# 27 unit pairs and three dense units in the grouped-query stage, two raw weight loads moved into the value stage, and the last quarter's order

## The chip, the core and the metric

The kernel runs on one NeuronCore of one Trainium2 chip. The metric is device time of one launch in microseconds (us). The engines are called as in the profile: PE is the matmul engine (its weight loads are PEld), DVE the vector engine, ACT the scalar (activation) engine, POOL the GpSimd engine, and SP the engine whose queue issues most DMAs. PSUM holds matmul results (8 banks of 128 x 512 float32), SBUF everything else.

## The reference

One encoder block over 1024 tokens of width 1024, in float32:

```
h = rms_norm(x, g_pre)
a_qkv, bq, bk, bv, mq, ga, gb, gm, mg = split(h @ w_in)
oa = three dilated sliding-window attentions (8 heads each), merged by their log-denominators
ob = grouped-query attention: 8 query heads over 2 key/value heads, qk rms-norm, axial rotary
om = cross-attention into 256 memory tokens
y_i = (o_i * silu(g_i)) @ w_br_i                      (i = a, b, m)
merged = sum_i sigmoid(mg_i + b_merge_i) * y_i
out = x + rms_norm(merged @ w_out, g_post)
```

The part of `w_in` that matters here is cut into *units*: 128 output columns, a 128 x 1024 block of raw weights. 24 units (`U_M`) make the merge gates `mg`, 12 (`U_G`) the silu gates, 24 the rotary queries and keys of the sliding-window branch.

## The kernel before, in words

Each float32 operand is split into two fp32r parts, high and low (`split`, lines 105 to 107: ACT copies the high part, DVE subtracts it to get the low part). A product is three matmul passes: high-high, high-low and low-high. `hh` and `hl` are the two parts of the normalised input for all 1024 tokens.

A unit can be computed in two ways:

- **Dense** (`dense`, lines 139 to 149, by `add_unit`): for each half of the tokens 8 blocks x 3 passes, so 48 matmuls of 512 columns a unit, with a raw load of 512 KB and one split. Dense units of the merge gates (`add_filler`) serve as filler inside attention stages: `weave` interleaves the unit's matmuls with those of the attention by a table of nominal costs, and gives the filler out evenly over the attention's cost. `FILL` lists which merge-gate units are done this way; the first runs in the cross-attention stage, the others (`FILL[1:]`) in the grouped-query stage.
- **In pairs**, by a Strassen-type scheme with seven products (lines 925 to 1395): two units are multiplied at once with seven products of 12 matmuls, 84 matmuls instead of 96. The operands are sums of halves of the raw weights (`weight_sum`: S1 to S4; POOL forms them, DVE for pair 1), their splits (`block_of`, `own_blocks`) and sums of halves of the input (T1 to T4, prepared in the value stage and split on the way, `split_block`). A pair needs both its raw weights, `BL[n][0]` and `BL[n][1]`, which `load_pair` fetches through SP's queue. Merge-gate units that are not in `FILL` come as the last pairs.

The stages follow each other on PE, whose order is fixed by the program: start and key/value projection, cross-attention with queries, the grouped-query stage ("B", lines 651 to 792), the value stage (16 steps and 28 steps of 12 matmuls, line 997), the pairs (line 1109), the sliding-window attention with the branch projections woven in (line 1312), and the output projection (line 1892), which again uses seven products (`prod_o`).

**Grouped-query stage.** It works on 16 items (8 token tiles x 2 key/value heads) of 8 steps each. Step n issues a row-maximum matmul (`row_max`, line 705) into one of three PSUM tiles `tr`, which DVE reduces (line 706); two steps after the last row of an item a small transpose (`shift`, line 713, with DVE line 714) brings the maxima into the score operand; twelve steps later come the scores (lines 723, 724), whose exponentials ACT writes to `bp` (line 726); POOL sums the eight `bp` tiles of an item one after the other (lines 728, 730); after the item's eighth score and two more, `pv` issues 16 matmuls of values (line 739), and one step later `final` sums the denominators with two matmuls (line 126) whose operands `blh` and `bll` are a split of POOL's sum by ACT and DVE. `q_prep` turns the next tile's queries (line 679), copied by ACT and DVE (lines 682 to 686), and uses a `tr` tile as well. ACT, DVE and POOL are ordered by a scheduler in this stage, PE by the program.

**From the value stage to the pairs.** From the value stage on all engines run in program order. `START` gives the first products: (0,1), (0,2), (0,4), (0,3), (1,1), (0,5), (1,4) and so on, where (n, x) is product x of pair n. `own_blocks(1)` splits pair 1's first raw weights for (1,1). The raw weights of pair 0 are loaded inside the value stage, both into `wr` tiles (two buffers); those of pair 1 after it, since the second one lies in memory of the pool `sr`, which replaces the value stage's pool `vp`. The value stage's results leave through `vr` tiles (seven buffers) and DMAs that SP and ACT issue.

**Last quarter.** Row block 3 ends the program: its first half of rows, (3,0), is scaled and sent by `send_part`, while product (3,"5") and the two 256-column cuts of product (3,"7") finish the second half, (3,1): `evac_o` and `piece(0)`, `piece(1)` bring them from PSUM (lines 1911 and 2052), ACT squares them (line 1904), and after mean (lines 1918, 1920) and POOL's root (line 1924) the last `send_part`s (line 1953) send them.

Of the kernel before, what the change touches and what calls it, by code (L numbers as in the profile page):

```python
# [8 lines left out]
F32 = mybir.dt.float32  # L9
# [6 lines left out]
S = 1024  # L16
NT = 8
P = 128
# [32 lines left out]
def block(ctx: ExitStack, tc: tile.TileContext, x, xT, memT, cst, msk, bcst, tabA, gpost,  # L51
          wu, wv, wb, wmem, wbr, wout, out):
    nc = tc.nc
# [4 lines left out]
    wp = ctx.enter_context(tc.tile_pool(name="wp", bufs=2))  # L58
# [749 lines left out]
    tbp, tb = pool("tb")  # L808
    tab = [tb.tile([P, S], F32, name=f"tab{j}") for j in range(2)]
    vpp, vp = pool("vp")  # L810
    t23p, t23 = pool("t23", "right")
# [11 lines left out]
    def rs():  # L823
        return vp.tile([P, 512], F32, name="vr", bufs=7)

# [22 lines left out]
    x_load(0)  # L848
    rl = vp.tile([P, 64], F32, name="rl")
    VR = {}  # L850
# [93 lines left out]
    def load_pair(n, u):  # L944
        if u == 0 or n == 0:
            BL[n][u] = wp.tile([P, 1024], F32, name="wr", bufs=WR)
        else:
            BL[n][u] = sr.tile([P, 1024], F32, name="rw", bufs=2)
        nc.sync.dma_start(BL[n][u], wu[pairs[n][1][u]])
# [36 lines left out]
    for n, (i, e, k) in enumerate(steps_v):  # L986
# [30 lines left out]
        if 6 <= n < 20 and n % 4 == 3:  # L1017
            x_blocks(n // 4 - 1)
            if n < 19:
                x_load(n // 4)  # L1020
        if n == 4:
            nc.sync.dma_start(rl, lbd.rearrange("h (a b) -> (h a) b", b=64))
        if n == 8:
# [14 lines left out]
        if n == FIRST + 16:  # L1038
            load_pair(0, 0)
            load_pair(0, 1)  # L1040
        if n == FIRST + 21:
            own_blocks(0)
# [25 lines left out]
    p1, v_, y_ = [sr.tile([P, 512], F32, name=f"sp{j}") for j in range(3)]  # L1068
    load_pair(1, 0)
    load_pair(1, 1)  # L1070
# [148 lines left out]
    def m_load(tile_):  # L1219
        nc.sync.dma_start(tile_, od[2, len(MB)])  # L1220
        MB.append(tile_)
# [7 lines left out]
    def tasks(n, x):  # L1229
# [8 lines left out]
        for m, nm in blocks:  # L1238
            block_of(m, nm)
        for nm, k in {(0, "1"): [("T2", 2), ("T2", 3)], (0, "2"): [("T3", 0)]}.get((n, x), ()):  # L1240
            split_block(nm, k)
        j = {(0, "2"): 1, (0, "4"): 2, (0, "3"): 3, (1, "4"): 4}.get((n, x))
        if j:
# [23 lines left out]
        if n == last - 1 and x in "46" or n == last and x == "1":  # L1267
            if x != "6":
                m_load(wp.tile([P, S], F32, name="wr", bufs=WR))
            if x != "1":  # L1270
                m_load(sr.tile([P, S], F32, name="rw", bufs=2))
        if n == last and x in "4352":
# [84 lines left out]
    for n, nm in order:  # L1357
        prod(n, nm)
        if (n, nm) == (0, "4"):
            own_blocks(1)  # L1360
            for j in (1, 2, 3):
                split_block("T3", j)
# [584 lines left out]
    def gain(n, u, c):  # L1947
        r = RES[n, u]
        V.tensor_tensor(r[:, c], r[:, c], gp[:, c], op=OP.mult)

    def send_part(n, u, c, queue_):
        T, r = n + 4 * u, RES[n, u]
        V.scalar_tensor_tensor(r[:, c], r[:, c], SS[n, u][:, 3:4], XT_[T][:, c], op0=OP.mult, op1=OP.add)
        queue_.dma_start(out[T * 128:T * 128 + 128, c], r[:, c])
# [91 lines left out]
    gain(3, 0, hi)  # L2046
    send_part(3, 0, lo, nc.sync)
    send_part(3, 0, hi, nc.sync)
    evac_o(*before)

    def piece(e):
        V.tensor_tensor(res[:, quarter[e]], d[e], u2[:, quarter[e]], op=OP.add)
        square(3, 1, 2 * e, res[:, quarter[e]])

    piece(0)
    gain(3, 1, hi)
    mean(3, 1, (1, 0))
    piece(1)
    gain(3, 1, quarter[0])
# [21 lines left out]
LA_T, LA_P = 2, 3  # L2081
FILL = (16, 17, 18, 19, 20, 21)
GATES = ((2, 2), (2, 3), (1, 0), (1, 1), (1, 2), (1, 3), (0, 0), (0, 1), (0, 2), (0, 3))
# [110 lines left out]
```

## Time and profile before

| what | before |
|---|---|
| median of 3 runs (lowest to highest) | 1412.65 us (1411.01 to 1413.41) |
| the profiled execution | 1410.94 us, span 1409.2 us |
| mean granted PE clock | 0.998 |
| PE busy | 1382.1 us, 98% of the span |
| DVE, ACT, POOL busy | 987.5, 678.9, 556.5 us |
| chain that ended last | PE 88%, DVE 5%, ACT 2%, issue 2% |
| grouped-query stage | about 218 to 438.5 us of the span |
| value stage | 438.5 to 558 us |
| pairs | 558 to 1057 us |
| sliding-window attention, output projection | 1057 to 1325 us, 1325 to 1409 us |

Times in the rows of the profile count from the span's start; the span leaves out 1.74 us of the profiled execution. PE's busy time overstates its work, since each matmul is shown with its whole passage (about 389 ns) while the next one follows after about 227 ns: the distance from start to start is what one costs. A small gap between two matmuls hides inside that overlap.

### The profile page before, as it was taken

Reading aid. Unit: us, or ns where it says so; the run is one execution under the profiler, and the core shown is the slowest. Engines: PE = TensorE matmul, PEld = TensorE weight load, DVE = VectorE, ACT = ScalarE, POOL = GpSimd, SP = SyncE. Lnnn points to the kernel's source line nnn. Section 1 sums busy time; section 2 is a strip of 40 time slices with the busy share of each in tenths; the row PEclk is TensorE's granted clock in tenths of the full one; section 3 lists DMA queues with packets and bytes.
Section 4 is the critical chain, followed back from the end, with each engine's and each line's share of the span. In section 5 each row is a group of like instructions: output and inputs, shape, how many; then the busy total and the mean of one; then the engine's idle time right before and its main releaser. Section 6 shows DMA issues by size and latency. Waiting matters only on the chain.

```text
span 1409.2 us, 21232 instructions
## 1 busy us (share of the span) xinstructions
PE 1382.1 (98%) x7487; PEld 1106.4 (79%) x7487; DVE 987.5 (70%) x1774; ACT 678.9 (48%) x1450; POOL 556.5 (39%) x437
## 2 busy tenths in 40 slices
PE   7999999999999999999999999999999999999997
PEld 7799986666666888788888888888887777777886
DVE  7765567677663387789787777755666666868977
ACT  6553355666653454544223222344456766742453
POOL 0515603766763422177455565423310011345410
PEclk9999999999999999999999999999999999999999
DMA  6342011011005673565455665665667576746613
GB/s 232 105 133 63 28 58 54 28 34 35 23 27 185 242 260 110 182 223 215 123 167 164 178 180 158 211 225 187 213 210 251 181 225 199 243 121 226 229 61 135
DMA packets 107067, 215.80 MB, mean 153 GB/s; under 512 B 19952, under 2 KB 49872, under 8 KB 106960
## 3 DMA queue, kind: packets, MB, share of 16 engines
q1 hardware_dynamic: 93184, 200.68, 44.2%
q10 hardware_dynamic: 13776, 13.77, 2.8%
q8 instruction: 59, 0.97, 0.3%
q14 instruction: 48, 0.39, 0.1%
HBM read 141.73 MB, written 60.09 MB: 143 GB/s over the span
## 4 chain that ended last, share of the span: by engine, by line
PE 88%; DVE 5%; ACT 2%; issue 2%; POOL 1%; DMA 1%; SPq 0%; POOLq 0%; ACTq 0%; DVEq 0%
PE s L1109 34%; PE d L1312 9%; PE s L997 6%; PE s L1892 4%; PE ov L739 4%; PE s L1479 3%; PE d L1542 3%; PE d L144 3%; PE d L146 3%; PE d L148 3%; PE tr L705 2%; PE s L723 2%; PE s L724 2%; PE d L997 2%; PE d L540 2%
## 5 line engine op out<-in xcount | busy, mean ns | idle before, releaser
L1109 PE MATMUL s<-T,ch 128*128 128x512 f32 x912 | 215.2, 389 | 1.7 <-ACT sp L1174 1.7
L1109 PEld LDWEIGHTS s<-T,ch 128*128 128x128 f32 x912 | 171.1, 188 | 37.7 <-ACT sp L1174 2.1
L730 POOL TENSOR_TENSOR bl<-bl,bp 128x512 f32<-128x512 f32 x96 | 123.7, 1288 | 48.5 <-ACT bp L726 42.5
L107 DVE TENSOR_TENSOR ch<-sf,ch 128x512 fp32r<-128x512 f32 x102 | 92.5, 914 | 62.7 <-ACT ch L106 62.6
L1109 PE MATMUL s<-hh,ch 128*128 128x512 f32 x408 | 129.8, 389 | 0.0
L1312 PE MATMUL d<-hh,wh 128*128 128x512 f32 x384 | 126.8, 399 | 1.0 <-DVE wl L1318 1.0
L706 DVE TENSOR_REDUCE bn<-tr 128x1 f32<-128x512 f32 x128 | 85.4, 686 | 19.6 <-PE tr L705 18.2
L726 ACT ACTIVATE bp<-s 128x512 f32<-128x512 f32 x128 | 76.0, 597 | 45.0 <-PE s L724 43.3
L1142 POOL TENSOR_TENSOR o<-o,rc 128x1024 f32<-128x1024 f32 x24 | 61.9, 2580 | 70.6 <-DMA o<-rs 48.3
L1109 PEld LDWEIGHTS s<-hh,ch 128*128 128x128 f32 x408 | 76.6, 188 | 15.9
L1174 ACT ACTIVATE sp<-s 128x512 f32<-128x512 f32 x52 | 31.1, 598 | 115.2 <-PE s L1109 94.5
L1312 PEld LDWEIGHTS d<-hh,wh 128*128 128x128 f32 x384 | 72.0, 188 | 17.2 <-DVE wl L1318 1.6
L1319 POOL TENSOR_TENSOR acc<-acc,wl 128x512 f32<-128x512 f32 x32 | 56.8, 1778 | 68.2 <-DVE wl L1318 68.0
L1109 PE MATMUL s<-hh,wl 128*128 128x512 f32 x208 | 81.0, 390 | 1.4 <-DVE wl L107 1.4
L1109 PE MATMUL s<-hl,wh 128*128 128x512 f32 x208 | 80.9, 389 | 0.0
L1109 PE MATMUL s<-hh,wh 128*128 128x512 f32 x208 | 80.9, 389 | 0.0
L1109 PE MATMUL s<-hl,ch 128*128 128x512 f32 x204 | 79.4, 389 | 0.0
L106 ACT ACTIVATE wh<-wr 128x1024 fp32r<-128x1024 f32 (+1 forms) x64 | 56.1, 878 | 46.9 <-PE d L1312 12.0
L144 PE MATMUL d<-hh,wh 128*128 128x512 f32 x192 | 76.6, 399 | 1.7 <-DVE fth L223 1.7
L1497 ACT ACTIVATE pra<-pra,sts 128x192 f32<-128x192 f32 (+2 forms) x176 | 77.4, 442 | 1.6 <-DVE sts L1489 1.6
L1312 PE MATMUL d<-hl,wh 128*128 128x512 f32 x192 | 77.8, 405 | 0.0
L146 PE MATMUL d<-hl,wh 128*128 128x512 f32 x192 | 76.6, 399 | 0.0
(422 smaller groups left out, 3596.9 us busy)
## 6 DMA issues: line engine op xcount, KB each, us to landing
wr<-in_wu SPq DMA_DIRECT2D x39, 512.0 KB, 6.4
rw<-in_wu SPq DMA_DIRECT2D x25, 512.0 KB, 4.9
o<-rs SPq DMA_DIRECT2D x96, 128.0 KB, 2.3
qkd<-o SPq DMA_DIRECT2D x24, 512.0 KB, 6.3
wl<-thd SPq DMA_DIRECT2D x24, 512.0 KB, 5.3
thd<-rs ACTq DMA_DIRECT2D x36, 256.0 KB, 2.7
aq<-qkd SPq DMA_DIRECT2D x12, 512.0 KB, 4.6
ak<-qkd SPq DMA_DIRECT2D x12, 512.0 KB, 6.0
```

The source lines that it names most:

```text
L107: V.tensor_tensor(dst_l, src, dst_h.bitcast(F32), op=OP.subtract)
L144: PE.matmul(dst, wh[:, k, :], hh[k][:, t], start=k == 0, stop=False)
L146: PE.matmul(dst, wh[:, k, :], hl[k][:, t], start=False, stop=False)
L706: fp["last"] = V.tensor_reduce(st[i]["n"][:, j, c:c + 1], s, axis=AX.X, op=OP.min)
L726: A.activation(pp, s, AF.Exp, scale=-1.0)
L730: G.tensor_tensor(lsum[i % 2], lsum[i % 2], pp, op=OP.add)
L997: PE.matmul(now[j], a, b, start=k == 0 and q == 0, stop=k == end and q == 2)
L1109: PE.matmul(dst, a, b, start=opens and i == 0, stop=closes and i == 11, skip_group_check=True)
L1142: G.tensor_tensor(QO[n, u], QO[n, u], RT.pop((n, u))[0], op=OP.add)
L1312: PE.matmul(s, a, b, start=q == 0, stop=q == 11)
L1319: G.tensor_tensor(accs[f][:, h], accs[f][:, h], th[:, h], op=OP.add)
L1497: A.activation(src, src, AF.Exp, scale=-1.0, bias=sums(T, h, 0), accum_out=sums(T, h, 1))
```

## The change

1. `FILL` loses two entries: three dense units remain in the grouped-query stage instead of five (the one in the cross-attention stage stays), and the two units that leave become a 27th pair.
2. A function `second_raw` gives the second raw weights of a pair one buffer in the pool `tb` (even pairs) or one in `sr` (odd pairs); `tb` is opened before the value stage's pool. Pair 0's second weights go there, and the freed `wr` buffer takes pair 1's first weights, so that three of the first four loads are issued inside the value stage (at step 32) and one after it. To make room, `vr` has six buffers instead of seven and the 64-column tile `rl` uses one of them.
3. In the first products of the pairs, all four splits of T3 are issued at (0,4), and pair 1's sums move: S1 from (0,2) to (0,4), S2 from (0,4) to (0,3), S3 from (0,3) to (1,1).
4. In the last quarter the second half's evacuation is issued ahead of the first half's two sends, the two pieces are put between and behind these, and the mean follows the second piece.

```
-        return vp.tile([P, 512], F32, name="vr", bufs=7)
+        return vp.tile([P, 512], F32, name="vr", bufs=6)
...
+    def second_raw(n):
+        return tb.tile([P, S], F32, name="rw0") if n % 2 == 0 else sr.tile([P, S], F32, name="rw1")
...
     def load_pair(n, u):
-        if u == 0 or n == 0:
-            BL[n][u] = wp.tile([P, 1024], F32, name="wr", bufs=WR)
-        else:
-            BL[n][u] = sr.tile([P, 1024], F32, name="rw", bufs=2)
+        BL[n][u] = second_raw(n) if u else wp.tile([P, 1024], F32, name="wr", bufs=WR)
         nc.sync.dma_start(BL[n][u], wu[pairs[n][1][u]])
...
         if n == FIRST + 16:
             load_pair(0, 0)
             load_pair(0, 1)
+            load_pair(1, 0)
...
-    load_pair(1, 0)
     load_pair(1, 1)
...
-        for nm, k in {(0, "1"): [("T2", 2), ("T2", 3)], (0, "2"): [("T3", 0)]}.get((n, x), ()):
+        for nm, k in {(0, "1"): [("T2", 2), ("T2", 3)], }.get((n, x), ()):
             split_block(nm, k)
-        j = {(0, "2"): 1, (0, "4"): 2, (0, "3"): 3, (1, "4"): 4}.get((n, x))
+        j = {(0, "4"): 1, (0, "3"): 2, (1, "1"): 3, (1, "4"): 4}.get((n, x))
...
         if (n, nm) == (0, "4"):
             own_blocks(1)
-            for j in (1, 2, 3):
+            for j in range(4):
                 split_block("T3", j)
...
     gain(3, 0, hi)
-    send_part(3, 0, lo, nc.sync)
-    send_part(3, 0, hi, nc.sync)
     evac_o(*before)
...
+    send_part(3, 0, lo, nc.sync)
     piece(0)
+    send_part(3, 0, hi, nc.sync)
     gain(3, 1, hi)
+    piece(1)
     mean(3, 1, (1, 0))
-    piece(1)
...
-FILL = (16, 17, 18, 19, 20, 21)
+FILL = (16, 17, 18, 19)
```

How this moves instructions is shown at three places. The first is PE at the start of the grouped-query stage, from the first row-maximum matmul (line 705); lines 144 to 148 are the dense filler. Before:

```order
L705 MATMUL tr<-KS,QH 128x512
L146 MATMUL d<-hl_99,wh 128x512
L148 MATMUL d<-hh_91,wl 128x512
L705 MATMUL tr<-KS,QH 128x512
L144 MATMUL d<-hh_92,wh 128x512
L146 MATMUL d<-hl_100,wh 128x512
L705 MATMUL tr<-KS,QH 128x512
```

Now:

```order
L705 MATMUL tr<-KS,QH 128x512
L148 MATMUL d<-hh_89,wl 128x512
L705 MATMUL tr<-KS,QH 128x512
L144 MATMUL d<-hh_90,wh 128x512
L705 MATMUL tr<-KS,QH 128x512
L146 MATMUL d<-hl_98,wh 128x512
L148 MATMUL d<-hh_90,wl 128x512
```

Between two row maxima there were two filler matmuls and are now one or two. Counted from the first query transposes to the value stage, PE has 239 filler matmuls before and 143 now: 47 and 28 up to the first value product (line 739), 160 and 96 from there to the fourteenth, 12 and 7 to the fifteenth, 20 and 12 after it.

The second place is DVE behind the end of the value stage (`T` are input halves, `ch` and `wl` low parts of weights, `sf` the weight sums of pair 1, `rs` an output). Before:

```order
L107 TENSOR_TENSOR ch<-sf_5629,ch 128x512
L107 TENSOR_TENSOR T_5401<-T_5401 128x512
L971 TENSOR_TENSOR sf_5627<-rw 128x512
L107 TENSOR_TENSOR wl<-wr,wh 128x1024
L107 TENSOR_TENSOR T_5401<-T_5401 128x512
L107 TENSOR_TENSOR T_5487<-T_5487 128x512 x2
L1154 TENSOR_TENSOR rs<-s_5652,sp_5620 128x512
```

Now:

```order
L107 TENSOR_TENSOR ch<-sf_5501,ch 128x512
L107 TENSOR_TENSOR wl<-wr,wh 128x1024
L107 TENSOR_TENSOR T_5275<-T_5275 128x512 x2
L107 TENSOR_TENSOR T_5361<-T_5361 128x512 x2
L1155 TENSOR_TENSOR rs<-s_5524,sp_5494 128x512
L1157 TENSOR_TENSOR rs<-rs,rb 128x512
L971 TENSOR_TENSOR sf_5499<-rw_5497 128x512
```

The sum that reads pair 1's second raw weights (`rw`) stands behind the output instead of ahead of the split `wl`.

The third place is DVE in the last quarter. Before:

```order
L1949 TENSOR_TENSOR res<-res,on_12601 128x512
L1953 SCALAR_TENSOR_TENSOR res<-res,hbm,on_12602 128x512 x2
L1911 TENSOR_TENSOR res<-s_13026,wr 128x512
L2052 TENSOR_TENSOR res<-s_13197,wr 128x256
L1949 TENSOR_TENSOR res<-res,on_12601 128x512
L1918 TENSOR_SCALAR hbm<-hbm 128x1
L1920 SCALAR_TENSOR_TENSOR hbm<-hbm 128x1
L2052 TENSOR_TENSOR res<-s_13198,wr 128x256
```

Now:

```order
L1950 TENSOR_TENSOR res<-res,on_12609 128x512
L1912 TENSOR_TENSOR res<-s_13034,wr 128x512
L1954 SCALAR_TENSOR_TENSOR res<-res,hbm,on_12610 128x512
L2051 TENSOR_TENSOR res<-s_13205,wr 128x256
L1954 SCALAR_TENSOR_TENSOR res<-res,hbm,on_12610 128x512
L1950 TENSOR_TENSOR res<-res,on_12609 128x512
L2051 TENSOR_TENSOR res<-s_13206,wr 128x256
L1919 TENSOR_SCALAR hbm<-hbm 128x1
```

The evacuation (line 1911 before, 1912 now) stands ahead of the two sends (line 1953 before, 1954 now), and the second piece ahead of the mean.

More of the change, by code (lines that the diff above doesn't have):

```diff
@@ L848, in block @@
     x_load(0)
-    rl = vp.tile([P, 64], F32, name="rl")
     VR = {}
@@ L1021, in block @@
         if n == 4:
+            rl = rs()[:, 0:64]
             nc.sync.dma_start(rl, lbd.rearrange("h (a b) -> (h a) b", b=64))
@@ L1270, in tasks @@
             if x != "1":
-                m_load(sr.tile([P, S], F32, name="rw", bufs=2))
+                m_load(second_raw(last + 1 if n < last and x == "4" else last + 2))
         if n == last and x in "4352":
```

## Prediction

> **What bounds the kernel now.** I read the chain of waits first, then a table of the stages.
>
> ```profile
> PE 88%; DVE 5%; ACT 2%; issue 2%; POOL 1%; DMA 1%; SPq 0%; POOLq 0%; ACTq 0%; DVEq 0%
> 218.40:438.50 220.10, 218.16 (x945) 135.66 (x944) 149.55 (x222) 128.93 (x220) 144.24 (x112) 1.00 0.11 33
> 558.10:575.40 17.30, 14.24 (x62) 11.15 (x60) 13.92 (x21) 8.89 (x16) 1.30 (x1) 1.00 0.59 178
> 575.40:1057.00 481.60, 481.58 (x2124) 398.57 (x2124) 356.71 (x419) 178.69 (x289) 227.27 (x138) 1.00 0.59 189
> ```
>
> The columns behind each stretch are its length and the busy time of PE, PEld, DVE, ACT and POOL, then the granted clock. PE is full in the pairs (third stretch) and nearly so in the grouped-query stage (first); 3 us are open in the passage between value stage and pairs (second). So the kernel pays for matmuls, and the change takes 12 away. But in the grouped-query stage DVE and POOL are busy for two thirds of the time. There the question is whether they can follow a PE that has less filler.
>
> **The price of a matmul.** Starts, in the chain of waits and in PE's order of time:
>
> ```profile
> 575.42 470.90 PE s L1109 x2076
> 425.71 0.39 PE L148 MATMUL d<-hh,wl 128*128 128x512 f32 x1
> 426.64 0.40 PE L723 MATMUL s<-QH,KS 128*128 128x512 f32 x1
> ```
>
> In the pairs one costs 470.90 / 2076 = 0.2268 us, so pair 27 adds 84 x 0.2268 = **19.05 us**. Its sums, splits and loads lie beside PE, as those of the other pairs do (481.58 busy of 481.60). In the grouped-query stage four fillers fill 426.64 - 425.71, which is 0.2325 each; the 96 that leave are worth at most 96 x 0.2325 = 22.3 us. If all of that came back, the move alone would gain 3.3 us. I take the stage in four pieces, by the counts of fillers given with the change.
>
> **Up to the first value product: 19 fillers, 4.4 us of PE.** The row maxima come first, and one needs a reduction on DVE.
>
> ```profile
> 217.39 0.59 ACT L683 ACTIVATE QH<-tr 64x512 fp32r<-64x512 f32 x1
> 218.62 0.40 PE L705 MATMUL tr<-KS,QH 128*128 128x512 f32 x1
> 218.60:239.00 20.40, 19.55 (x84) 14.32 (x82) 19.39 (x31) 8.62 (x15) 7.26 (x6) 1.00 0.12 39
> 239.10 3.58 PE ov L739 x16
> ```
>
> From the first row maximum to the first value product DVE is busy for 19.39 of 20.40 us. The fillers that leave were covering DVE, not holding it up. DVE's work stays (22 reductions, four query corrections, two shifts, one filler's output). The row maxima can start 218.62 - 217.98 = 0.6 us earlier, when the query copy that they read ends. At least 0.4 of that arrives, since the first two reductions then wait for two query corrections and the third for the `tr` tile that these hold. At most DVE's 1.0 us of idle time goes too, and 0.5 since the product doesn't wait for the last 0.68 us reduction: 2.1. I take the middle, **1.3 us** earlier (0.4 to 2.1). Three of 4.4 us are lost here.
>
> **From there to the fourteenth: 64 fillers, 14.9 us.** Thirteen cycles of (410.11 - 239.10) / 13 = 13.15 us lose 4.9 fillers each and become 12.0 us.
>
> ```profile
> 410.11 3.58 PE ov L739 x16
> L730 POOL TENSOR_TENSOR bl<-bl,bp x96: 1261/1287/1600, 232.7 to 434.9; 128x512 f32<-128x512 f32 x96
> 239.00:410.10 171.10, 170.56 (x746) 106.41 (x747) 122.92 (x181) 105.64 (x179) 117.28 (x92) 1.00 0.11 31
> 256.09 0.69 DVE L107 TENSOR_TENSOR bll<-bl,blh 128x512 fp32r<-128x512 f32 x1
> 258.52 0.39 PE L126 MATMUL tr<-bll,one 128*1 128x512 f32 x1
> ```
>
> No engine is full at 12.0 us: POOL needs 7 x 1.29 = 9.0, DVE 122.92 / 13 = 9.5, ACT 8.1 a cycle. What can stop PE is the tail of POOL's sum: `bll`, the last link, is ready at 256.78, and its matmul starts at 258.52, a slack of 1.74 us in a cycle with a query copy. The five fillers that leave take at most 1.16 of it, 0.58 stays. So the cycles keep nearly all; for waits behind the remaining fillers' DVE work I give back 0.5 us in all: **14.4 us** (12 to 14.9).
>
> **The drain: 5 + 8 fillers.** The five up to the fifteenth product are on PE's path, 1.1 us. Behind it no row maxima are left and POOL sets the end:
>
> ```profile
> 421.86 3.58 PE ov L739 x16
> 427.31 0.60 ACT L726 ACTIVATE bp<-s 128x512 f32<-128x512 f32 x1 [0.86 <-PE s L724]
> 428.05 8.11 POOL L730 TENSOR_TENSOR bl<-bl,bp 128x512 f32<-128x512 f32 x6 [0.84 <-ACT bp L726]
> 437.60 0.39 PE L126 MATMUL tr<-bll,one 128*1 128x512 f32 x1 [0.33 <-DVE bll L107]
> 438.52 0.40 PE L997 MATMUL s<-wh,hh 128*128 128x512 f32 x1
> ```
>
> Exponential, six sums, split: 10.2 us that no filler shortens, and PE already waits for them. Of eight fillers (1.9 us) only the two ahead of that exponential and the one behind the last matmul count, 0.7 us, and less if POOL is still at the item before: **0.5 us** (0.3 to 0.7); PE will idle about 1.9 us at 437.6. The value stage starts 1.3 + 14.4 + 1.1 + 0.5 = **17.3 us** earlier (13.8 to 18.8) for a pair that costs 19.05: this half of the change loses 1.75 us.
>
> [...]
>
> **The passage to the pairs.** Pair 1's first weights come too late:
>
> ```profile
> 547.66 14.11 SPq L908 DMA_DIRECT2D vdr<-vr  x8
> 561.86 5.28 DMA wr<-in_wu
> 567.22 1.06 ACT L106 ACTIVATE wh<-wr 128x1024 fp32r<-128x1024 f32 x1 [0.18 <-DMA wr<-in_wu]
> 569.86 1.22 DVE L107 TENSOR_TENSOR wl<-wr,wh 128x1024 fp32r<-128x1024 f32 x1
> 569.17 0.39 PE L1109 MATMUL s<-hh,wh 128*128 128x512 f32 x1
> 571.13 0.50 PE L1109 MATMUL s<-hh,wl 128*128 128x512 f32 x1 [1.35 <-DVE wl L107]
> 571.00 1.89 DVE L107 TENSOR_TENSOR T<-T 128x512 fp32r<-128x512 f32 x3
> 572.81 0.68 DVE L1154 TENSOR_TENSOR rs<-s,sp 128x512 f32<-128x512 f32 x1
> 575.42 5.78 PE L1109 MATMUL s<-T,ch 128*128 128x512 f32 x24 [1.73 <-ACT sp L1174]
> 566.55 0.69 DVE L107 TENSOR_TENSOR ch<-sf,ch 128x512 fp32r<-128x512 f32 x1 [0.23 <-ACT ch L106]
> ```
>
> The load is issued at 561.86 behind eight stores on SP; PE starts (1,1) at 569.17 and waits for `wl`, then waits for the copy `sp`, which stands in ACT's and DVE's order behind the T splits and an output (572.81). With the load inside the value stage the split follows `ch` (566.55): ACT's `wh`, 1.06 us behind ACT's part of `ch`, ends near 567.5, `wl` at 568.65, four T splits of 0.6 at 571.05, the output there instead of at 572.81, and the copy frees (0,5) the same 2.61 us later, at 573.66 instead of 575.42. (1,1) would end at 569.17 + 12 x 0.2268 = 571.9, so the first wait goes and a second of 1.75 stays, for the same copy: **1.8 us** (0 to 3.5). The sum that reads the later raw weights has passed behind that output and finds them landed. The extra 512 KB load inside the value stage goes ahead of T loads on SP; PE is full there and the splits stand two steps (5.4 us) ahead of use, so I count it as nothing; uncovered it would be some 2 us.
>
> **The end.**
>
> ```profile
> 1398.53 0.60 ACT L1980 ACTIVATE wr<-s 128x512 f32<-128x512 f32 x1 [1.21 <-PE s L1892]
> 1398.70 1.42 DVE L1953 SCALAR_TENSOR_TENSOR res<-res,hbm,on 128x512 f32<-128x512 f32 x2 [0.44 <-POOL hbm L1924]
> 1400.04 0.68 DVE L1911 TENSOR_TENSOR res<-s,wr 128x512 f32<-128x512 f32 x1
> 1401.51 0.69 DVE L1949 TENSOR_TENSOR res<-res,on 128x512 f32<-128x512 f32 x1 [0.46 <-ACT d L1904]
> 1402.45 0.42 DVE L2052 TENSOR_TENSOR res<-s,wr 128x256 f32<-128x256 f32 x1
> 1403.75 0.67 POOL L1924 TENSOR_TENSOR hbm<-hbm,mhalf 128x1 f32<-128x1 f32 x1 [5.08 <-DVE hbm L1920]
> 1388.81 12.55 PE L1892 MATMUL s<-w,hl 128*128 128x512 f32 x66
> ```
>
> The last matmul ends at 1401.36, the second piece follows only at 1402.45: DVE does sends, the evacuation, a gain and two means first. Now the evacuation can start at 1398.55, and the sends fill the wait for PE. One send (0.7) and a gain (0.6) behind the first piece (1400.0 to 1400.4) put the second piece at 1401.7, and square, root and sends follow: **0.75 us** (0 to 1.0).
>
> **Sum.** 19.05 - 17.3 - 1.8 - 0.75 = -0.8 us. The profiled execution took 1410.94, 1.7 below the median of the runs (1412.65); its own time would become 1410.1, the median **1411.8 us**. With every bound on one side the sum goes from -4.25 to +5.25 us.
>
> **Rivals.**
> 1. PE decides everywhere: the start and the drain of the grouped-query stage follow the fillers too, 22.3 us instead of 17.3. Then 1412.65 + 19.05 - 22.3 - 1.8 - 0.75 = 1406.85. For it speaks PE's 218.16 of 220.10, against it DVE's 19.39 of 20.40.
> 2. The sum of the denominators becomes the cycle: `bll` later than its matmul in the thirteen cycles. It decides once POOL and the copies run 0.58 us later within a cycle than now; each 0.3 us beyond that costs 13 x 0.3 = 3.9. At 0.5 us a cycle: 1411.8 + 6.5 = 1418.3. Against it: engines with a quarter of each cycle free.
> 3. Neither passage nor end gives anything, since the same copy `sp` or the last store is waited for anyway: 1412.65 + 1.75 = 1414.4.
>
> **How the numbers follow.** Forecast 0.58, rivals 0.17, 0.12 and 0.13. A change under 0.2% (2.8 us) can't be told from none by a measurement of this kernel. Faster than 1409.8 are rival 1 and the low edge of the forecast (0.09): 0.26. Slower than 1415.5 are rival 2 and an edge of rival 3: 0.15. The rest, 0.59, is no change. The range for 8 in 10 is 1408.3 to 1415.3: it leaves out most of rivals 1 and 2.
>
> **What would show it.** Right: the first value matmul (line 997 before) moves from 438.5 to about 421; up to the first value product (now near 237.8) PE shows new waits for DVE's reductions; the cycles behind it are near 12.0 us; a wait of about 2 us for `bll` at the end; in the passage one wait instead of two; the pairs last 19 us longer; the tail from the last matmul to the end is 0.75 us shorter. Wrong: cycles above 12.3 (rival 2), or a value stage that starts before 418.5 (rival 1).

## The result, and the profile after

| | before | after |
|---|---|---|
| median (lowest to highest), 21 runs each | 1412.52 us (1410.52 to 1415.6) | 1414.01 us (1413.3 to 1415.69) |
| the profiled execution | 1410.94 us, span 1409.2 | 1415.69 us, span 1413.6 |

The ratio is 1.0013, 95% interval 1.0007 to 1.0019: the change makes the kernel 1.5 us slower (1.0 to 2.7). The forecast was 0.8 us less than before; 1414.01 lies inside the range that was given (1408.3 to 1415.3), but the sum had the wrong sign. The two profiled executions lie near opposite ends of their kernels' runs (4.4 us apart in span, where the medians are 1.5 apart), so each kernel was profiled once more. The table of the changed kernel's stages, by windows; the columns are those of the prediction's stretches:

```profile
217.54:423.47 205.93, 201.36 (x853) 116.84 (x853) 141.69 (x216) 124.07 (x215) 144.79 (x112) 1.00 0.09 25
423.47:544.53 121.06, 121.06 (x529) 100.17 (x529) 72.82 (x95) 55.52 (x89) 33.28 (x23) 0.99 0.65 222
544.53:560.02 15.49, 13.77 (x62) 11.08 (x60) 13.35 (x20) 8.62 (x16) 0.34 (x1) 1.00 0.52 161
560.02:1060.60 500.58, 500.58 (x2208) 414.55 (x2208) 365.31 (x433) 186.76 (x302) 234.27 (x142) 1.00 0.58 186
1060.60:1329.30 268.70, 265.58 (x2071) 208.64 (x2071) 192.22 (x586) 156.17 (x524) 71.78 (x40) 1.00 0.65 208
1393.73 12.55 PE L1893 MATMUL s<-w,hl 128*128 128x512 f32 x66
```

These are the grouped-query stage from its first row maximum, the value stage, the passage, the pairs from product (0,5) on, and the sliding-window stage; the last row is PE's last run of matmuls. Both executions of both kernels (the second ones belong to the two repeats below):

| us | before | before again | after | after again | mean difference | forecast |
|---|---|---|---|---|---|---|
| value stage's first matmul, from the span's start | 438.52 | 438.17 | 423.47 | 423.69 | -14.8 | -17.3 |
| value stage | 119.77 | 120.72 | 121.06 | 119.83 | +0.2 | 0 |
| passage, to (0,5) | 17.13 | 17.22 | 15.49 | 15.49 | -1.7 | -1.8 |
| pairs, to the sliding-window stage | 481.58 | 481.55 | 500.58 | 500.62 | +19.0 | +19.05 |
| sliding-window stage | 267.4 | 267.5 | 268.7 | 268.5 | +1.2 | 0 |
| rest of the span | 84.8 | 84.7 | 84.3 | 84.4 | -0.4 | -0.75 |
| span | 1409.2 | 1409.9 | 1413.6 | 1412.5 | +3.5 | -0.8 |

So the pair costs what it was said to cost and the passage gives what it was said to give. The grouped-query stage gives 2.5 us too little, and two stages that the sum held at nothing, the value stage and the sliding-window stage, show something of their own. The spans of these four executions differ by 3.5 us, the medians by 1.5; both executions of the kernel before that were profiled lie below its median, both of the changed kernel above its own.

**The drain.** PE's and POOL's order of time in the changed kernel, in the last of the grouped-query stage's work:

```profile
412.90 8.05 POOL L730 TENSOR_TENSOR bl<-bl,bp 128x512 f32<-128x512 f32 x6
420.07 0.40 PE L144 MATMUL d<-hh,wh 128*128 128x512 f32 x1
421.67 0.39 PE L126 MATMUL tr<-blh,one 128*1 128x512 f32 x1 [1.21 <-ACT blh L106]
422.40 0.39 PE L126 MATMUL tr<-bll,one 128*1 128x512 f32 x1 [0.34 <-DVE bll L107]
423.47 0.79 PE L997 MATMUL s<-wh,hh 128*128 128x512 f32 x1
424.06 0.63 PE L997 MATMUL s<-wh,hl 128*128 128x512 f32 x1
```

PE waits 1.21 + 0.34 us, first for the high part of POOL's sum, where about 1.9 us of idling were foretold. What follows was not: the value stage's first matmuls start 0.59 us apart instead of 0.23.

```profile
423.40:424.40 1.00, 1.00 (x3) 0.83 (x3) 0.82 (x2) 1.00 (x4) 0.00 (x0) 0.50 0.14 33
424.40:425.40 1.00, 1.00 (x4) 0.72 (x3) 1.00 (x2) 1.00 (x3) 0.00 (x0) 0.50 0.06 14
425.40:426.50 1.10, 1.10 (x5) 0.86 (x4) 0.95 (x3) 0.71 (x2) 0.00 (x0) 0.64 0.22 49
```

The third column from the end is the granted clock: 0.50 from 422.8 to 426.2 us by the trace's clock records. From these shares I estimate that 0.5 + 0.5 + 1.1 x 0.36 = 1.4 us of matmul time are lost in these three windows.

### The profile page after: what moved, and what is told of

Its sections match the earlier page's. It is cut to its first block, busy times and chain, and to the rows that moved or that the text cites. A ratio compares the mean times of both kernels' runs of the same rounds, so it can differ in the third digit from the quotient of the medians.

```text
span 1413.6 us, 21233 instructions
## 1 busy us (share of the span) xinstructions
PE 1386.2 (98%) x7475; PEld 1105.2 (78%) x7475; DVE 989.1 (70%) x1781; ACT 681.4 (48%) x1457; POOL 562.5 (40%) x441
## 4 chain that ended last, share of the span: by engine, by line
PE 83%; DVE 6%; ACT 3%; POOL 3%; issue 2%; DMA 2%; SPq 0%; ACTq 0%; POOLq 0%; DVEq 0%
PE s L1110 35%; PE d L1313 8%; PE s L997 6%; PE s L1893 4%; PE ov L739 3%; PE s L1480 2%; PE d L1543 2%; PE d L148 2%; PE d L144 2%; PE d L997 2%; PE d L146 2%; PE s L723 2%; PE d L540 2%; PE tr L705 2%; PE s L724 2%
## 5 line engine op out<-in xcount | busy, mean ns | idle before, releaser
L1110 PE MATMUL s<-T,ch 128*128 128x512 f32 x948 | 223.6, 390 | 1.7 <-ACT sp L1175 1.7
L1110 PEld LDWEIGHTS s<-T,ch 128*128 128x128 f32 x948 | 177.9, 188 | 39.0 <-ACT sp L1175 2.1
L1110 PE MATMUL s<-hh,ch 128*128 128x512 f32 x424 | 135.0, 389 | 0.0
L1313 PE MATMUL d<-hh,wh 128*128 128x512 f32 x384 | 127.1, 400 | 1.1 <-DVE wl L1319 1.0
L1110 PE MATMUL s<-hh,wh 128*128 128x512 f32 x216 | 84.1, 390 | 0.0
L1110 PE MATMUL s<-hl,wh 128*128 128x512 f32 x216 | 84.1, 390 | 0.0
L1110 PE MATMUL s<-hl,ch 128*128 128x512 f32 x212 | 82.6, 390 | 0.0
L1313 PE MATMUL d<-hl,wh 128*128 128x512 f32 x192 | 77.9, 406 | 0.0
L107 DVE TENSOR_TENSOR wl<-wr,wh 128x1024 fp32r<-128x1024 f32 x37 | 48.1, 1303 | 35.5 <-ACT wh L106 35.4
L1638 POOL TENSOR_TENSOR og<-og 128x1024 f32<-128x1024 f32 (+1 forms) x9 | 18.5, 2055 | 132.8 <-DVE og L1635 132.8
```

The costliest lines, as they stand in the source:

```text
L107: V.tensor_tensor(dst_l, src, dst_h.bitcast(F32), op=OP.subtract)
L1110: PE.matmul(dst, a, b, start=opens and i == 0, stop=closes and i == 11, skip_group_check=True)
L1313: PE.matmul(s, a, b, start=q == 0, stop=q == 11)
```

## Experiment: the two halves apart

Edit 1, on the kernel before (the two units leave the grouped-query stage, nothing else). "Six" and "four" dense units, here and in the expectations, count the one in the cross-attention stage.

```
-FILL = (16, 17, 18, 19, 20, 21)
+FILL = (16, 17, 18, 19)
```

> The kernel before with one edit: FILL loses two entries, so 27 pairs and three dense units, everything else as before. Theory A (from the trace of the change: the grouped-query stage gives back only some 13.7 of 22.3 us, and PE's granted clock halves for 3.5 us after the wait at that stage's end): the move costs 19.05 - 13.7, less what the start of a run varies, so about +4 us against the kernel before, near 1416.5. Rival (the forecast's sum for this half, 17.3 us back): +1.75, near 1414.3. The trace should show about 0.5 granted clock at the first matmuls of the value stage under A, 1.00 under the rival.

Measured, in five runs: 1417.37 us, ratio 1.0039 (1.0026 to 1.0051), 5.5 us slower. The stages repeat the changed kernel's: value stage from 423.46, with the clock at 0.99 on the mean over its 121.03 us as in the changed kernel's 121.06, and the kernel before's passage of 17.20.

Edit 2, on the changed kernel (everything but the units):

```
-FILL = (16, 17, 18, 19)
+FILL = (16, 17, 18, 19, 20, 21)
```

> The changed kernel with FILL as before (six entries, 26 pairs): only the early raw weights with their buffers, the moved sums and the last quarter's order. Both theories expect the passage to the pairs to give 1.6 to 1.8 us and the end up to 0.75, so about 2.4 us faster than the kernel before, near 1410.1. Rival: these waits are replaced by others behind them and the time stays at 1412.5; then the move of the units costs only 1.5 us.

Measured: 1413.12 us, ratio 1.0008 (0.9999 to 1.0016): no gain. The passage is as short as forecast (15.5), but the value stage takes 122.18 us instead of 119.77. Who waits there, SP's order, and then ACT's and PE's:

```profile
SPq L858 <- DMA thd<-fth: 8.3, 1, 8.3
...
445.05 0.38 SPq L215 DMA_DIRECT2D thd<-fth  x1
453.84 1.76 SPq L858 DMA_DIRECT2D vA<-in_wv  x4
...
491.18 2.39 ACT L842 ACTIVATE wr<-wr,cs 128x1024 f32<-128x1024 f32 x2 [8.24 <-DMA wr<-in_xT]
493.48 0.61 ACT L106 ACTIVATE wh<-vA 128x512 fp32r<-128x512 f32 x1
...
494.14 0.50 PE L997 MATMUL s<-wh,hh 128*128 128x512 f32 x1 [1.14 <-ACT wh L106]
```

SP stands 8.3 us behind the store of a filler's output (`thd<-fth`) before it issues the next load of value weights. Behind that stands the loop that prepares the sums of the input: load `wr<-in_xT`, scaling on ACT (line 842), four subtractions on DVE, four stores on SP, next load. The whole loop comes later, and ACT, which works in order, scales at 491.18 what it scales 2.7 us earlier in a version without this wait (below); the split `wh` that PE needs is next behind it. The cause stands in the program: here the load into the third weight tile waits for the store's semaphore (`DMAHW2`), so the tile must lie on the buffer that is being stored. In the trace SP's wait ahead of that load is for the semaphore that the store's landing updates.

```
L215 DMA thd<-fth 128x512 [waits DMAHW2_49,Activation_49]
L858 DMA vA_4670<-in_wv 128x1024 [waits DMAHW2_49,DMAHW3_49,PE_49,Pool_49]
```

In the kernel before, and in the changed one, the same load has no such wait. The change makes `tb` larger by the new buffer, `vp` smaller by one `vr` buffer and by `rl`, so tiles come to lie elsewhere; which of these moved the weight tile, no run shows. With six dense units the move lands a load on a buffer in flight; with four it does not. The clock falls in this execution too, behind the passage (0.67 on the mean from 575 to 580): the pairs take 483.23 us instead of 481.58. So the halves (+5.5 and +1.2) don't add up to +1.5: the second half alone pays for a wait on SP that the whole change doesn't have.

## Experiment: the gap at the drain

Two ways to fill PE's wait. The first puts eight matmuls behind the last value product whose result nobody reads:

```
+                    if m == 127:
+                        z = pss1()
+                        for _ in range(DUMMY):
+                            PE.matmul(z, KS[:, 0, 0:128], QQ[7][0][:, 0:4], start=True, stop=True)
```

> The changed kernel with eight more matmuls whose result nobody reads, behind the last value product of the grouped-query stage, where PE waits for POOL anyway; no filler moves. Theory A (the wait lets the granted clock fall, and the first 3.5 us of the value stage run at half): the wait is filled, the clock stays at 1.00 and 1.7 us come back, near 1412.3. Rival (the clock fell only in the one execution that was profiled, or costs nothing): 1414.0, as the changed kernel.

Measured: 1416.86 us, ratio 1.0034 (1.0023 to 1.0044). The clock does not fall in the value stage of the profiled execution (1.00 on the mean), and yet the kernel is some 3 us slower than the changed one. The value stage takes 121.70 us, with waits for `wh` again. SP's order, first of the changed kernel, then of this one:

```profile
415.82 0.52 SPq L832 DMA_DIRECT2D sum<-in_wv  x1
425.97 0.59 SPq L832 DMA_DIRECT2D sum<-in_wv  x1
426.60 0.43 SPq L838 DMA_DIRECT2D wr<-in_xT  x1
```

```profile
425.43 0.52 SPq L836 DMA_DIRECT2D sum<-in_wv  x1
426.72 0.43 SPq L836 DMA_DIRECT2D sum<-in_wv  x1
427.20 0.89 SPq L842 DMA_DIRECT2D wr<-in_xT  x2
```

The first 512 KB load of the stage, which came at 415.82, now comes at 425.43. So all of the stage's loads crowd together, and the last scaling ends 54.7 us into the stage instead of 52.1. This run therefore says nothing on the clock's price.

The second way takes fillers from the cycles and puts them behind the last value product, by a higher nominal cost of that step (13 instead of 3 between the product and the denominators' matmuls):

```
-                    yield 8 * 432
+                    yield 8 * 432 + (DRAIN if m == 127 else 0)
...
+DRAIN = 14000
```

(the stage's total cost `B_COST` grows by the same).

> The changed kernel with 14000 more in the cost table at the last value product of the grouped-query stage, so that 13 filler matmuls instead of 3 stand between it and the denominators' matmuls, taken evenly from the stage ahead (2 from the start, 8 from the cycles). Theory A: 1.7 us from the clock and 1.6 us from the filled wait, near 1410.7, below both kernels. Rival (DVE and POOL set the cycles, so that taking fillers out of them gives nothing): only the clock's 1.7, near 1412.3.

Measured: 1412.21 us, ratio 1.0001 (0.9992 to 1.0010), 1.8 below the changed kernel by the medians. PE's order of time behind the last value product:

```profile
413.25 3.65 PE L739 MATMUL ov<-bp,VS 128*64 128x512 f32 x16
...
419.71 0.39 PE L144 MATMUL d<-hh,wh 128*128 128x512 f32 x1
419.93 0.39 PE L126 MATMUL tr<-blh,one 128*1 128x512 f32 x1
420.16 0.39 PE L126 MATMUL tr<-bll,one 128*1 128x512 f32 x1
...
237.27:393.17 155.90, 154.81 (x674) 92.37 (x673) 115.49 (x176) 100.64 (x173) 116.85 (x92) 1.00 0.08 21
```

No wait is left at the drain, the thirteen cycles take 155.90 / 13 = 11.99 us, and the value stage starts at 420.86: ten fillers are hidden, 10 x 0.2325 = 2.3 us. The fall of the clock is gone from the head of the value stage (its first matmuls start at 420.86, 421.09 and 421.33); in this execution one stands behind the passage, where PE waits 1.7 us for ACT (0.80 on the mean from 555 to 560; the pairs take 502.25 us instead of 500.6). The median lies at the rival's 1412.3, but the rival's reason is not borne out: the cycles did give time when fillers left them.

## Experiment: both kernels once more, and the last quarter alone

> The changed kernel as it is, one more profiled execution. If the fall of the granted clock at the head of the value stage belongs to the kernel, it stands there again (0.5 for 3 to 4 us from 422 on, 1.7 us lost) and every stage repeats to 0.3 us: 1415 to 1416. If it hangs on the phase of the gap against something that runs on its own, it is gone or at another place (the passage to the pairs), and the time moves with it: 1413.3 to 1414 without it.

Measured: 1414.28 us. PE's order and the clock where it had fallen:

```profile
421.89 0.39 PE L126 MATMUL tr<-blh,one 128*1 128x512 f32 x1 [1.23 <-ACT blh L106]
422.62 0.39 PE L126 MATMUL tr<-bll,one 128*1 128x512 f32 x1 [0.34 <-DVE bll L107]
...
423.60:424.60 1.00, 0.91 (x4) 0.78 (x5) 1.00 (x2) 1.00 (x4) 0.00 (x0) 1.00 0.15 33
424.60:425.60 1.00, 1.00 (x6) 0.82 (x5) 0.88 (x2) 1.00 (x3) 0.00 (x0) 1.00 0.05 11
```

The same gap to 0.02 us, and no fall: the value stage takes 119.83 us instead of 121.06, so the execution with the fall has the stage 1.2 us longer. The other stages repeat to 0.3 us, the longer sliding-window stage with them.

The first profile of the changed kernel around its fall, and around its wait in the passage (behind the stretch stand its length and PE's busy time, third from the end the granted clock):

```profile
419.38:422.79 3.41, 1.87 (x8) 0.92 (x7) 1.14 (x2) 1.22 (x2) 1.50 (x2) 1.00 0.00 0
422.79:426.20 3.41, 3.41 (x10) 2.19 (x9) 2.63 (x5) 3.28 (x6) 0.00 (x0) 0.50 0.13 29
556.61:560.02 3.41, 1.69 (x9) 1.07 (x7) 3.22 (x6) 1.17 (x3) 0.00 (x0) 1.00 0.00 0
560.02:563.43 3.41, 3.41 (x15) 2.84 (x16) 2.59 (x5) 1.83 (x4) 0.00 (x0) 1.00 0.68 204
```

In the 3.41 us ahead of the fall PE is busy for 1.87; in the 3.41 us up to the end of the wait in the passage it is busy for 1.69, and the clock stays at 1.00 behind it. Why the wait at the drain is followed by a fall in this execution and not in the repeat, and the wait in the passage by none in either, was not shown.

> The kernel before as it is, one more profiled execution. If value-stage waits and clock falls are matters of one execution, this one may show either (each costs 1 to 2 us: 1412.5 to 1414 instead of 1410.9); if they belong to the changed kernels alone, it repeats the first profile in every stage to 0.3 us, with a value stage of 119.8 us and no fall of the clock ahead of 1400: 1410.5 to 1411.5.

Measured: 1411.69 us. No fall (1.00 in every stage up to 1325 us), but a value stage of 120.72 us instead of 119.77, with a wait of 0.5 us for the same `wh`, here for its low part on DVE. The kernel before stands at the edge of that wait too.

The last quarter's new order alone, on the kernel before (item 4 of the change):

> The kernel before with the last quarter's new order alone (the two sends put between the two pieces, the second piece ahead of the mean). Theory (the order gives the 0.4 to 0.5 us that the spans show behind the last matmul of the output projection): 7.6 to 7.7 us from that matmul to the end instead of 8.1, the rest as before, median 0.4 to 0.5 lower, ratio 0.9995 to 1.0000. The prediction's own term was 0.75. Rival (the difference of 0.4 is the chance of one execution): 8.1 again, no difference.

Measured: 1412.53 us, ratio 0.9999 (0.9990 to 1.0008). From the end of PE's last run of matmuls to the end of the span it takes 1408.3 - 1400.94 = 7.36 us, as in the changed kernel (7.36 and 7.37), against 7.79 in both executions before. So the order gives 0.43 us, which the median can't show.

## Experiment: the loop of the value stage

If the loop of loads, scalings and subtractions is a second bound of the value stage, then a faster loop should help. The first attempt, on the kernel with six dense units and the other edits, issues the first of the next two loads as soon as two of the four subtractions have read its buffer:

```
             V.tensor_tensor(to[j], x, y, op=OP.subtract)
+            if j == 2 and k < 3:
+                XT[0] = wp.tile([P, S], F32, name="wr", bufs=WR)
+                nc.sync.dma_start(XT[0], xT[k + 1])
             nc.sync.dma_start(tsd[j, k], to[j])
+        if k < 3:
+            XT[1] = wp.tile([P, S], F32, name="wr", bufs=WR)
+            nc.sync.dma_start(XT[1], xT[k + 5])
```

> The kernel with the other edits but six dense units in the grouped-query stage (26 pairs), with one edit in the value stage: of the next two 512 KB loads of the scaled input the first is issued as soon as two of the four block subtractions have read its buffer, not behind all four stores. Theory (the value stage has a second bound close to the matmuls': load, scaling on ACT, four subtractions on DVE, four stores, next load, and the ACT split queued behind the scaling makes the matmuls wait): each of the three turns of that loop gets 1 to 2 us shorter, the waits on the line of the value products (1.1 and 0.45 us in the run without this edit) are gone, the stage is 119.5 to 120.0 us long instead of 122.2, and the whole is the kernel before less 1.6 (passage) and 0.5 (end): about 1410, ratio 0.998 to 0.999. Rival A (the waits come from the smaller number of value output buffers or from the reciprocal's tile in one of them): the waits stay at 1 us or more, 1412.5 to 1413.5. Rival B (they are chance of one execution): no waits, but the median stays at 1413.

Measured: 1415.36 us, ratio 1.0016 (1.0008 to 1.0025): worse than any of the three expected. ACT's scalings, and PE's wait:

```profile
489.06 1.15 ACT L842 ACTIVATE wr<-wr,cs 128x1024 f32<-128x1024 f32 x1 [5.81 <-DMA wr<-in_xT]
493.02 1.15 ACT L842 ACTIVATE wr<-wr,cs 128x1024 f32<-128x1024 f32 x1 [2.80 <-DMA wr<-in_xT]
494.08 0.61 ACT L106 ACTIVATE wh<-vA 128x512 fp32r<-128x512 f32 x1
...
PE s L1003 <- ACT wh L106: 2.4, 1, 2.4
```

The two loads now land about 4 us apart, and only the later one counts, since `wh` stands behind both scalings. The last scaling ends 56.4 us into the stage instead of 55.2, PE's longest wait grows from 1.14 to 2.4 us, and the clock falls in the stage (0.99 on the mean over its 124.25 us, 1.00 in the run before). So the edit made the loop longer, not shorter, and PE waited longer with it: that speaks for the loop as a bound, and against this edit as the remedy. SP's 8.3 us behind the store were untouched (8.5 here).

The second attempt takes that wait away. It reserves the eight tiles of the subtractions ahead of the four weight tiles, so that a tile that is written later lies on the buffer in flight:

```
+    vv = [vp.tile([P, 512], F32, name=f"vv{j}") for j in range(4)]
+    vy = [vp.tile([P, 512], F32, name=f"vy{j}") for j in range(4)]
     VR = {}
...
-    vv = [vp.tile([P, 512], F32, name=f"vv{j}") for j in range(4)]
-    vy = [vp.tile([P, 512], F32, name=f"vy{j}") for j in range(4)]
```

> The kernel with the other edits and six dense units (26 pairs), with the eight tiles of the subtractions reserved ahead of the weights' four, so that another tile lies on the buffer whose store to DRAM is still under way at the head of the value stage. Theory (in the run without this edit the fifth load of the value weights lay on that buffer, and SP stood 8.3 us behind the store, with the loads of the scaled input queued behind it): no such wait on SP, the last of the sixteen subtraction stores is issued at most 57 us after the stage's first matmul instead of 59.0, the stage takes 119.7 to 120.2 us instead of 122.2, and with the passage's 1.6 and the end's 0.3 to 0.5 the kernel comes out 1.5 to 2 us below the kernel before: ratio 0.9986 to 0.9993. Rival (the smaller number of value output buffers or the extra load is what costs): the stage stays at 121.5 to 122.5 us, ratio 1.0005 to 1.001.

Measured: **1408.97 us** (1408.56 to 1410.52), ratio 0.9979 (0.9969 to 0.9989), 3.0 us below the kernel before and some 5 below the changed one, more than the 1.5 to 2 expected.

```profile
444.96 0.39 SPq L215 DMA_DIRECT2D thd<-fth  x1
445.59 3.97 SPq L860 DMA_DIRECT2D vA<-in_wv  x4
...
488.44 2.40 ACT L842 ACTIVATE wr<-wr,cs 128x1024 f32<-128x1024 f32 x2 [6.38 <-DMA wr<-in_xT]
490.74 0.61 ACT L106 ACTIVATE wh<-vA 128x512 fp32r<-128x512 f32 x1
...
438.01:557.86 119.85, 119.85 (x529) 99.04 (x528) 71.82 (x95) 55.67 (x90) 29.88 (x20) 1.00 0.64 225
```

The weight load follows the store at once, the scaling ends 2.7 us earlier than without the edit, and PE is full over the whole stage. One edit took the wait and the stage's 2.3 us away together, so the wait is their cause. The gain over the kernel before is only in part accounted for: the passage gives 1.7 us and the end 0.4, and in the two profiles the sliding-window stage takes 1.7 back (269.0 us against 267.4); their spans differ by 0.9 us, the medians by 3. What the kernel before loses in the executions that were not profiled is open.

The profiled executions without a fall of the clock in this stage, by the end of the last scaling (counted from the stage's first matmul):

| execution | last scaling ends | value stage |
|---|---|---|
| after again, last quarter alone, before | 52.4, 52.5, 52.7 | 119.83, 119.68, 119.77 |
| subtraction tiles first, the same with eight units | 52.8, 52.8 | 119.85, 119.82 |
| fillers at the drain, without and with unread matmuls in the passage | 53.3, 53.3 | 120.30, 120.33 |
| before again | 53.7 | 120.72 |
| subtraction tiles first, with unread matmuls in the passage | 54.0 | 121.03 |
| unread matmuls at the drain, other edits alone | 54.7, 55.2 | 121.70, 122.18 |

Up to some 52.8 us PE sets the stage's 119.8; past it each microsecond costs about one.

Both better versions were also run with eight unread matmuls in PE's wait in the passage, to see whether the clock then holds there:

```
+        if (n, nm) == (0, "5"):
+            z = psd()
+            for _ in range(WARM):
+                PE.matmul(z, hh[0][:, 0:128], hh[1][:, lo], start=True, stop=True)
         prod(n, nm)
```

> The run above with eight matmuls whose result nobody reads put ahead of the first product's thirteenth matmul in the passage to the pairs, into the 1.7 us in which the matmuls wait for ACT there. Theory (a wait of 1.7 us in that place lets the granted clock fall to about a half for 3 to 4 us in some executions): no fall at the passage, the passage not longer than 15.7 us, median 0.3 to 1.0 below the run above. Rival (falls come without regard to this wait): falls at the passage or elsewhere as before, median within 0.3 of the run above or above it by the matmuls' length that finds no cover (up to 0.2).

> The changed kernel (27 pairs) with the ten fillers moved behind the last value product and the eight unread matmuls in the passage. Theory (clock falls at the passage make the difference between the executions of the run with the moved fillers at 1410.5 to 1411.1 and those at 1413.3 to 1415.0): all executions near the lower group, median 1410.5 to 1411.5, ratio 0.9990 to 0.9998. Rival (the spread comes from late transfers in the value and sliding-window stages): the spread stays, median 1412 to 1412.5.

Measured: 1409.68 us with six units (ratio 0.9982, 0.9974 to 0.9991) and 1411.42 with four and the fillers at the drain (0.9995, 0.9986 to 1.0004). In the passage the matmuls cost nothing (15.4 and 15.5 us). With six units the median is 0.7 above the run without them, where 0.3 to 1.0 below was expected. The second run is tighter than the one without them, 1410.6 to 1412.6 instead of 1410.5 to 1415.0; the first is not, and in its profiled execution (mean clock 0.997, against 0.999 in that of the run without them) two matmuls of the sliding-window stage stand 0.59 us apart at 1155.81. That the matmuls help is not shown.

## Experiment: the step the other way

The fastest version with eight dense units in all and 25 pairs:

```
-FILL = (16, 17, 18, 19, 20, 21)
+FILL = (16, 17, 18, 19, 20, 21, 22, 23)
```

With 25 pairs the last of the eight operand steps that hang on the pairs behind the queries (three loads, two DVE products and a store for the next stage) has no pair to hang on and is left out; the times are read for the two stages alone.

> The fastest kernel so far (six dense units, the other edits, the subtractions' tiles first) with the step taken the other way: eight dense units in the grouped-query stage and 25 pairs. Theory (with six the matmuls already decide every cycle of that stage and its drain, so that two units more cost their full 96 matmuls of 0.2325 us, while two fewer gave back 14.6): the stage 22 to 23 us longer, the pairs 19.0 to 19.1 shorter, in all 3 to 4 us above the run with six, 1412 to 1413. Rival (something other than the matmuls still decides part of the stage with six, so that part of the new work is hidden): the stage less than 19 us longer, and the kernel as fast as that with six or faster.

Measured: 1411.97 us, ratio 0.9999 (0.9990 to 1.0008). The value stage starts at 458.17 instead of 438.01, 20.2 us later, and the pairs take 462.57 us instead of 481.59, 19.0 less. The stage's price lies between the two expectations, 0.21 us a matmul, so a little is hidden even here. Two units more cost 20.2, two fewer gave back 14.5 to 14.8, and a pair is worth 19.0: by these stage times six is the best of the three counts, by about 1 us on the one side and 4 on the other.

## Why the prediction was right and wrong

**Pair 27: right.** 19.05 forecast, 19.0 measured in both executions.

**The grouped-query stage: the term that failed.** Against 17.3 us stand 14.5 between the two second executions (14.8 in the mean of both). That shortfall alone turns the forecast's -0.8 us into about +2. By the prediction's pieces:

- Up to the first value product: 238.73 before, 237.72 after, 1.0 us. Forecast 1.3 (0.4 to 2.1).
- Thirteen cycles: from 170.98 to 158.69 us, 12.3 instead of 14.4. "So the cycles keep nearly all" is the step that failed: of 64 fillers' 14.9 us not 0.5 but 2.6 were lost, 12.2 us a cycle instead of 12.0. The prediction looked for one link that could become the cycle; no link did, `bll` least of all, so rival 2 fell. The loss is in short waits that the fillers had covered, for DVE's reductions and shifts and ACT's `bp` (rows below). The run with ten fillers moved to the drain shows that 11.99 a cycle were to be had, but with fewer fillers than the change left there.
- To the fifteenth product: 1.03 forecast as 1.1.
- The drain: 0.15 instead of 0.5. POOL's sum sets its end, as said, and the freed PE time became a wait.

PE's waits in the thirteen cycles, before and then after (what waits, for whom, us in total, times, longest):

```profile
PE tr L705 <- DVE bn L706: 0.4, 1, 0.4
```

```profile
PE tr L705 <- DVE bn L706: 0.6, 1, 0.6
PE s L723 <- ACT bp L726: 0.4, 1, 0.4
PE tr L713 <- DVE bnm L708: 0.3, 1, 0.3
```

These are the waits that show as idle time, 0.9 us more. The rest hides in the overlap of the shown matmuls: counted by the starts of matmuls that follow later than 0.26 us, the cycles hold 2.5 us more than before, 1.3 at the two score matmuls (lines 723 and 724), 0.8 at the shifts (line 713) and 0.4 at the row maxima (line 705).

Rival 1 (all 22.3 come back) fell for the reason given against it. POOL's sums of line 730 have a median of 1282 ns in the changed kernel and 1287 before. The longest of them, in the changed kernel, took 2.16 us; it started 0.2 us behind a split `wl` (128x1024) on DVE, which took 1.23 us there as at 215.83, where no sum runs:

```profile
273.38 1.23 DVE L107 TENSOR_TENSOR wl<-wr,wh 128x1024 fp32r<-128x1024 f32 x1
273.57 2.16 POOL L730 TENSOR_TENSOR bl<-bl,bp 128x512 f32<-128x512 f32 x1
```

In the kernel before, where a sum started 0.08 us ahead of the split (at 294.5), the sum took 1.30 us and the split 2.30. So in these two cases the one that started first kept its length and the other took about 1 us longer. There are only a few splits of weights in the stage, and the cycle in which the long sum ends took 12.0 us, less than the mean of 12.2: it does not explain the 2.6 us.

**The passage: right.** 1.7 instead of 1.8, and as said one wait goes and the second stays:

```profile
560.02 2.34 PE L1110 MATMUL s<-T,ch 128*128 128x512 f32 x9 [1.72 <-ACT sp L1175]
```

Rival 3 fell with that; that its 1414.4 us lies next to the measured 1414.0 is chance, since both passage and end gave time.

**The end: little more than half of it.** 0.43 instead of 0.75; the mechanism held, the size was off.

**What the sum did not hold.** First the granted clock: the gap at the drain was foretold and priced at nothing beyond its length, but behind it the clock stood at 0.50 for 3.41 us in one execution of the changed kernel and at 1.00 in the other, and the value stage was 1.2 us longer in the first. Second the sliding-window stage, 1.2 us longer in both profiles. Its difference sits in two places; the larger one, by ACT's order in the kernel before and after:

```profile
1149.09 1.06 ACT L106 ACTIVATE hh<-ot 128x1024 fp32r<-128x1024 f32 x1 [0.37 <-DMA ot<-od]
```

```profile
1154.54 1.06 ACT L106 ACTIVATE hh<-ot 128x1024 fp32r<-128x1024 f32 x1 [2.18 <-DMA ot<-od]
```

A load lands some 2 us later against the matmuls, ACT's exponentials queue behind the split, and PE loses 0.95 us there (0.42 in the repeat). It is late in both executions after (2.18, 1.70) and in neither before (0.37, 0.16). Neither half has it alone: with the units alone ACT waits 0.91 us and PE loses nothing, with the other edits alone 1.40 and 0.16. In the fastest version it is 2.57, and PE loses 1.3. So the loss follows the load's lateness; why the load is late, no run shows. Third, "I count it as nothing" for the extra load and what makes room for it: in the changed kernel that holds, but the same edits with six units cost 2.4 us, by where a tile came to lie. With that tile moved, the second half of the change is worth 3 us by the medians, without the first.

With the measured terms the spans come out as 19.0 - 14.8 - 1.7 - 0.4 + 1.2 + 0.2 = +3.5. The medians say +1.5. That the kernel before loses in its other executions what its second profile begins to show (0.95 in the value stage) would fit, and so would the small spread of the fastest version; it is argued, not shown, since only two of its executions were profiled. The prediction held that less than 2.8 us can't be told from none; 21 runs of each kernel did tell 1.5.

## What to carry to other kernels

Filler that left the stage here returned its length only where PE set the pace (1.03 of 1.1 us to the fifteenth product); where other engines stand a microsecond behind, expect some of it to stay as short waits (0.2 us a cycle here), and put the filler that remains where a chain of another engine leaves PE idle. When an edit changes tile counts or pools, look in the program for new waits of loads on stores that are still under way, and for what is queued behind them: here one such wait outweighed the gain that the edit was made for. Test the halves of a change apart, and profile each kernel twice before a difference of 2 us is read.

## What the runs showed of the hardware

A wait of PE of 1.21 and 0.34 us, with one matmul between, was followed by a granted clock of 0.50 for 3.41 us (422.79 to 426.20) in the changed kernel's profile, and by none in its repeat, with the same wait to 0.02 us; with the units alone the value stage behind it had 0.99 on the mean as well. Behind the wait in the passage (1.73 us before, 1.72 in the changed kernel, 1.58 with eight dense units) the clock fell in two profiles (the other edits alone, 0.67 on the mean from 575 to 580; the fillers at the drain, 0.80 from 555 to 560) and stayed at 1.00 in five (both kernels, the repeat of each, eight dense units). PE was busy for 1.87 of the 3.41 us ahead of the fall of the changed kernel's profile, and for 1.69 of the 3.41 us up to the end of its wait in the passage, with no fall, so this share alone did not decide; what did, no run shows.

With the other edits alone the load that waits for a store's semaphore stood on SP until the store had landed, 8.3 us, and what stood behind it on SP's queue was issued after it (453.84); with the subtraction tiles first the same load followed the store at once (445.59).
